# A decoder layer on one core: the build-time scheduler holds loads back and lets urgent operations pass, the first norm's weight vector is spread on chip, and the last tiles are transposed as they become final

## The chip, the cores and the metric

The kernel runs on one core of one Trainium2 chip. The metric is the device time of one execution in microseconds (us), as the median of three runs: 2298.27 (2297.4 to 2301.95). Lower is better.

## The reference

One layer of a hybrid decoder in float32. 16 learned meta tokens stand ahead of 1024 tokens; D = 1024, the feed-forward width is 2816, and there are 8 attention heads and 8 RWKV-7 heads of 64.

```python
h = concatenate([meta, x])                                   # 1040 x 1024
n = rms_norm(h, ffn1_norm);  h = h + 0.5 * (silu(n @ wg1) * (n @ wu1)) @ wd1
n = rms_norm(h, mix_norm);   p = n @ w_in                    # q,k,v and the RWKV columns
h = h + concatenate([stick_breaking_attention(p), rwkv7_time_mix(p)]) @ w_out
n = rms_norm(h, ffn2_norm);  h = h + 0.5 * (silu(n @ wg2) * (n @ wu2)) @ wd2
return rms_norm(h, final_norm)[16:]                          # x * rsqrt(mean(x^2) + eps) * gain
```

The RWKV recurrence is sequential over tokens; the kernel computes it in chunks, and each chunk needs the inverse of small lower triangular blocks.

## The kernel before

**Tiling.** Activations stand transposed: features on the 128 partitions, tokens along the row. The tokens are two groups, A (16 + 512) and B (512), and each group two chunks of 256 or 272 columns. The stages are ffn1, the input projection with attention and RWKV, `w_out`, ffn2 and the final norm; group B's ffn1 is woven into group A's mixing, and so on, so that TensorE always has some dense product at hand. Every dense product is three matmuls (`mm3`): activations and weights are each split into a high part (rounded to fp32r) and the rest, and high x high, low x high and high x low are added in PSUM. So each weight block is loaded (`wraw`, 512 KB on SP's queue, two buffers), copied to `whi` on ACT and subtracted to `wlo` on DVE. In the names of the profile `pg` and `pu` are the gate and up products, `pd` the down product, `pwo` that with `w_out`, `nh` and `nl` the high and low part of a normed activation, `ah` and `al` those of the feed-forward's inner activation.

**What sets the order.** While the program is built, a list scheduler inside the kernel (class `Clock`) plays it through with costs of its own. The stages are generators with priorities. A TensorE operation is issued as its generator comes to it; operations of DVE, ACT, POOL and the DMA issues of SP go into one pending list per engine, and `catch_up` takes, of all those whose inputs are there, the one with the smallest key: its earliest start first, and then its level (URGENT, LOAD, PLAIN, LAZY, set by `with self.urgent()` and the like). What is written out is one fixed order per engine; on the chip each engine works through its own in that order, and waits where an input is late. `self.dma` is the time until which the played DMA queue is full, `self.port` that until which DVE or POOL holds the memory port which the two share.

**Start** (`xfirst`, `startup`, `block`). The first two blocks of 128 tokens are loaded, then the vector `ffn1_norm`, as a DMA that copies it to all 128 partitions (`g1b`, 512 KB). ACT squares and sums each block, DVE makes the inverse root (`bst`) and one operation per block multiplies by root and vector (`xn`), TensorE transposes it in 16 pieces (`pxn`), ACT and DVE split them (`nh`, `nl`), and the first gate product can run.

**The triangular solve** (`lanes`, eight times in the kernel, once per piece of RWKV work). The 16 x 16 blocks go out to memory and come back with one block per partition (`Ld`, `lt`); POOL inverts them in 15 steps of two operations (`ltmp<-lt,T` and `T<-T,ltmp`); the inverse goes out (`Td`, `Nd`) and comes back by 16 DMAs of a few KB (`t<-Td`, `tt<-Nd`) as blocks of larger matrices; TensorE then combines them in four rounds of small matmuls, `pw`, `pp`, `pz`, `pe`, with evictions by ACT and DVE between. `pG` (line 1411, in `prep`) are products of 128 x 128 that a later part of a piece's work takes.

**Norm sums** (`norm_add`, `norm_sums`). After each finished tile of 128 features ACT squares it (`nsq`), DVE adds it to `nacc`; the square of the last tile is not added but summed by TensorE from its own matmuls. `nps` (middle) and `fss` (end) are these matmuls with a matrix of ones.

**The end** (`last` in `ffn`, `hookE`, `final`). The last down products are made for feature tiles m = 0 to 7; tiles 4 to 7 of the last chunk come last of all. Then `final` takes the sums, makes the inverse root (`fst`), transposes all 16 pieces of the chunk back (`po<-ident,h2B`), and DVE multiplies each 128 x 512 half row by root and gain (`gfb`, a broadcast of `final_norm`) into `ot`, which is stored, 256 KB at a time.

## Time and profile before

| what | before |
|---|---|
| median of three runs | 2298.27 us (2297.4 to 2301.95) |
| the profiled execution: own time | 2300.61 us |
| its span in the trace | 2298.3 us |
| TensorE busy | 2244.2 us, 98% |
| DVE / ACT / POOL busy | 69% / 46% / 30% |
| mean DMA rate | 113 GB/s |

Engines in the rows: PE is TensorE's matmuls and PEld its weight loads; DVE, ACT and POOL are the vector, scalar and GpSimd engines; SP issues the DMAs. Nearly every operation is recorded by one helper and so carries its line, L99; a row is told by the names of the tiles, `out<-in`, with buffer numbers left out. A duration in brackets at a row's end is the time that the engine stood idle before it, and behind the arrow what ended that. An fp32 matmul that is not fp32r appears as two rows' worth of records (two instructions are "x4"). PEclk is the clock that TensorE was granted, as a share of 2.4 GHz.

### The profile page before, as it was taken

How to read it: one execution, taken by the hardware profiler on the slowest of the kernel's cores; microseconds unless marked ns; L12 is line 12 of the kernel's file. 1: busy time of each engine (PE TensorE's matmuls, PEld its weight loads, DVE VectorE, ACT ScalarE, POOL GpSimd, SP SyncE). 2: the span in 40 equal slices, each digit the busy share in tenths (PEclk: the TensorE clock that was granted, in tenths of full speed). 3: DMA queues.
4: the chain of work that ended last, by engine and by line, in shares of the span. 5: the costliest groups of instructions: out<-in, count | busy, mean ns of one | idle time of the engine just before them, and what ended most of it. 6: DMA issues, size and time to landing. Idle time of an engine off the chain costs nothing.

```text
span 2298.3 us, 41595 instructions
## 1 busy us (share of the span) xinstructions
PE 2244.2 (98%) x16339; PEld 1986.8 (86%) x16339; DVE 1579.3 (69%) x2605; ACT 1067.1 (46%) x2115; POOL 700.0 (30%) x786
## 2 busy tenths in 40 slices
PE   7999999999999999999999979999999999999998
PEld 7999999999878788778778977887877898898998
DVE  5788776585666655666576887646777566788775
ACT  5444444444444434555434545445666333344442
POOL 0255541003142231441012324413544011255540
PEclk9999999999999999999999989999999999999999
DMA  4642332545743232332546533324231533333322
GB/s 140 195 117 76 108 111 67 153 138 138 214 129 95 70 103 82 111 90 74 157 140 196 144 92 101 90 81 133 67 91 57 159 106 115 97 102 104 107 87 80
DMA packets 412103, 259.68 MB, mean 113 GB/s; under 512 B 45060, under 2 KB 396500, under 8 KB 411908
## 3 DMA queue, kind: packets, MB, share of 16 engines
q1 hardware_dynamic: 411908, 257.04, 38.4%
q8 instruction: 128, 2.10, 0.4%
q14 instruction: 67, 0.55, 0.1%
HBM read 222.99 MB, written 33.99 MB: 112 GB/s over the span
## 4 chain that ended last, share of the span: by engine, by line
PE 88%; DVE 6%; DMA 2%; ACT 2%; issue 1%; SPq 0%; DVEq 0%; ACTq 0%
PE pd L99 33%; PE pu L99 20%; PE pg L99 19%; PE pwo L99 3%; PE px L99 3%; PE po L99 2%; PE pz L99 2%; PE pat L99 2%; DVE wlo L99 2%; DVE ql L99 1%; PE pG L99 1%; ACT whi L99 1%; DVE cc L99 1%; PE psw L99 0%; SPq L99 0%
## 5 line engine op out<-in xcount | busy, mean ns | idle before, releaser
L99 ACT ACTIVATE whi<-wraw 128x1024 fp32r<-128x1024 f32 (+1 forms) x318 | 334.8, 1053 | 360.1 <-PE pd L99 222.9
L99 DVE TENSOR_TENSOR wlo<-wraw,whi 128x1024 fp32r<-128x1024 f32 (+1 forms) x318 | 425.9, 1340 | 102.5 <-ACT whi L99 98.9
L99 PE MATMUL pd<-ah,whi 128*128 128x512 f32 (+2 forms) x944 | 326.2, 346 | 1.4 <-DVE h L99 1.2
L99 PE MATMUL pd<-al,whi 128*128 128x512 f32 (+2 forms) x944 | 319.0, 338 | 2.1 <-DVE al L99 2.0
L99 PE MATMUL pd<-ah,wlo 128*128 128x512 f32 (+2 forms) x944 | 319.3, 338 | 0.0
L99 PE MATMUL pd<-nh,whi 128*128 128x256 f32 (+7 forms) x648 | 210.5, 325 | 1.6 <-DVE st L99 1.6
L99 PE MATMUL pu<-nh,whi 128*128 128x512 f32 (+3 forms) x584 | 210.1, 360 | 0.0
L99 PE MATMUL pd<-nh,wlo 128*128 128x256 f32 (+7 forms) x648 | 205.1, 316 | 0.4 <-DVE wlo L99 0.4
L99 PE MATMUL pd<-nl,whi 128*128 128x256 f32 (+7 forms) x648 | 205.2, 317 | 0.0
L99 PE MATMUL pu<-nh,wlo 128*128 128x512 f32 (+3 forms) x584 | 201.1, 344 | 4.1 <-DVE wlo L99 4.1
L99 PE MATMUL pg<-nh,whi 128*128 128x512 f32 (+3 forms) x544 | 200.9, 369 | 0.0
L99 PE MATMUL pu<-nl,whi 128*128 128x512 f32 (+3 forms) x584 | 200.5, 343 | 0.0
L99 PEld LDWEIGHTS pd<-ah,whi 128*128 128x128 f32 x944 | 177.7, 188 | 23.8 <-issue 2.9
L99 POOL TENSOR_TENSOR al<-sl,ah 128x512 fp32r<-128x512 f32 (+2 forms) x47 | 77.8, 1655 | 389.5 <-ACT ah L99 384.2
L99 PEld LDWEIGHTS pd<-al,whi 128*128 128x128 f32 x944 | 177.8, 188 | 20.7 <-DVE al L99 3.5
L99 PEld LDWEIGHTS pd<-ah,wlo 128*128 128x128 f32 x944 | 177.7, 188 | 20.5
L99 PE MATMUL pg<-nh,wlo 128*128 128x512 f32 (+3 forms) x544 | 191.4, 352 | 0.8 <-DVE wlo L99 0.8
L99 PE MATMUL pg<-nl,whi 128*128 128x512 f32 (+3 forms) x544 | 191.6, 352 | 0.2 <-DVE nl L99 0.2
L99 DVE SCALAR_TENSOR_TENSOR h<-pd,h 128x256 f32<-128x256 f32 (+1 forms) x200 | 107.2, 542 | 68.2 <-PE pd L99 66.0
L99 PEld LDWEIGHTS pd<-nh,whi 128*128 128x128 f32 (+2 forms) x648 | 120.2, 186 | 14.4 <-issue 3.2
L99 POOL TENSOR_TENSOR qs<-wraw 128x512 f32<-128x512 f32 x60 | 93.5, 1559 | 117.9 <-DVE ql L99 41.3
L99 PEld LDWEIGHTS pd<-nh,wlo 128*128 128x128 f32 (+2 forms) x648 | 120.3, 186 | 9.3 <-DVE wlo L99 0.6
(379 smaller groups left out, 5759.3 us busy)
## 6 DMA issues: line engine op xcount, KB each, us to landing
wraw<-in_ffn_w_gate_dram SPq DMA_DIRECT2D x92, 512.0 KB
wraw<-in_ffn_w_up_dram SPq DMA_DIRECT2D x92, 512.0 KB
wraw<-in_ffn_w_down_dram SPq DMA_DIRECT2D x88, 512.0 KB
wraw<-in_w_in_dram SPq DMA_DIRECT2D x54, 512.0 KB
wraw<-in_w_out_dram SPq DMA_DIRECT2D x18, 512.0 KB
s<-rkvd SPq DMA_DIRECT2D x18, 256.0 KB
raw<-qkvd SPq DMA_DIRECT2D x16, 264.0 KB
raw<-qkvd SPq DMA_DIRECT2D x16, 256.0 KB
```

The lines of the kernel that those rows point to most:

```text
L99: self._c.trace(self._n, op, lambda: f(*a, **k), out, [x for x in args if isinstance(x, bass.AP)], k)
```

## The change

It has six parts.

1. *Scheduler.* In `catch_up` a DMA's key is now at least `self.dma - 3.0`: a transfer is held in the pending list until the played queue is nearly empty, so that one that turns up later can still go ahead of it. And every operation of the urgent level has 0.1 taken off its key, so that it goes ahead of one that could start a little sooner.
2. *RWKV's transfers are urgent*: `s<-rkvd`, `tw`, `Ld`, `lt`, `Td`, `Nd`, `t<-Td`, `tt<-Nd`.
3. *Start.* `ffn1_norm` is loaded as one row (4 KB), two fp32 matmuls with ones spread it over the partitions, and two DVE copies make `g1b`. For the first two blocks DVE multiplies the block by `g1b` while ACT still sums squares, and by the root afterwards (`TENSOR_SCALAR`); the second block's transposes take two more PSUM banks. A one-column `Square` on ACT comes first of all.
4. *Gain of the final norm* is one of the per-feature vectors, `vec`, and ACT multiplies `h` by it in place, after squaring (32 more ACT operations of 128 x 256); the load of `gfb` is gone, and the output of the other chunks is scaled on ACT (`final`).
5. *The last chunk* has `final_last`: a tile's two transposes are issued as it becomes final, the squares of its last three tiles are summed by TensorE rather than added on DVE, and the output goes as two DMAs of 128 x 1024, half of each scaled on DVE and half on ACT. Two of the PSUM banks of ffn2's last phase are set aside for it (8 to 6).
6. `norm_sums` waits for each of its sources just before it is used.

```diff
-                    key = (max(t, c, self.port if o.port else 0.0), o.prio)
+                    key = (max(t, c, self.port if o.port else self.dma - BACKLOG if e == "s" else 0.0)
+                           - AHEAD * (o.prio[0] == -self.URGENT), o.prio)      # AHEAD = 0.1, BACKLOG = 3.0
...
-                if s["k"] == KT - 1 and now and not s["tile"]:
-                    s["last"] = sq
+                if s["k"] >= KT - s["late"] and now and not s["tile"]:
+                    s["last"].append(sq)
...
-        yield self.need(*src, bank=next or self.nextbank)
+        yield self.need(*src[:1], bank=next or self.nextbank)
         ps = bank(name)
         for i, x in enumerate(src):
+            if i:
+                yield self.need(x)
...
-                nc.scalar.activation(xn, xt, AF.Square, accum_out=st[:, 0, j:j + 1])
+                nc.scalar.activation(hot[j] if hot else xn, xt, AF.Square, accum_out=st[:, 0, j:j + 1])
+                if hot:
+                    nc.vector.tensor_tensor(out=xn, in0=xt, in1=self.g1b, op=ALU.mult)
...
+                if hot:
+                    nc.vector.tensor_scalar(out=xn, in0=xn, scalar1=st[:, 2, j:j + 1], scalar2=None, op0=ALU.mult)
+                else:
+                    nc.vector.scalar_tensor_tensor(xn, xt, st[:, 2, j:j + 1], self.g1b[0:m], ALU.mult, ALU.mult)
...
-        for r, c, l in blks:
-            nc.sync.dma_start(out=Ld[l].rearrange("l s t -> s l t"), in_=ab[r, :, c])
+        with self.urgent():
+            for r, c, l in blks:
+                nc.sync.dma_start(out=Ld[l].rearrange("l s t -> s l t"), in_=ab[r, :, c])
...
+    def final_last(self, s, h2, cs, bank, early):
...
+        for m in range(KT):
+            yield lambda: s()["k"] > min(max(m, m // 4 * 6), KT - 1)
+            yield self.need(h2[:, m, cs])
+            for b in range(2):
+                if m % 4 == 0:
+                    if m:
+                        yield self.need(bank=self.nextbank)
+                    pts.append((bank if m else early)("po"))
+                    self.hold(pts[-1:])
+            for b in range(2):
+                nc.tensor.transpose(out=pts[m // 4 * 2 + b][:, m % 4 * P:m % 4 * P + P], in_=h2[:, m, cs.start + b * P:cs.start + b * P + P],
+                                    identity=self.ident)
+        st, _ = yield from self.norm_sums(s(), 256, "fss", bank)
+        yield lambda: hasattr(self, "fo")
+        for b in range(2):
+            ot = self.fo.tile([P, D], F32, name="ot%d" % b)
+            with self.urgent():
+                nc.vector.tensor_scalar(out=ot[:, 0:512], in0=pts[b], scalar1=st[:, 1, b:b + 1], scalar2=None, op0=ALU.mult)
+                nc.scalar.activation(ot[:, 512:D], pts[2 + b], AF.Copy, scale=st[:, 1, b:b + 1])
+                nc.sync.dma_start(out=self.out[0, 512 + cs.start + b * P:512 + cs.start + b * P + P, :], in_=ot)
...
             with self.urgent():
+                nc.sync.dma_start(out=g1r, in_=A["ffn1_norm"])
                 xs.extend(xload(0, *b) for b in blks[:2])
-                nc.sync.dma_start(out=self.g1b, in_=A["ffn1_norm"][0].partition_broadcast(P))
+                nc.scalar.activation(g1w, self.ones[:, 0:1], AF.Square)
+            for q in range(2):
+                yield self.need(g1r, bank=self.tbank)
+                ps = tb("pg1")
+                nc.tensor.matmul(ps, lhsT=self.ones[0:1, :], rhs=g1r[:, 512 * q:512 * q + 512], start=True, stop=True)
+                with self.urgent():
+                    nc.vector.tensor_copy(out=self.g1b[:, 512 * q:512 * q + 512], in_=ps)
...
+                if gain:
+                    x = hh[:, m, slice(*ch[i])]
+                    nc.scalar.activation(x, x, AF.Copy, scale=self.v(gain, m))
```

Since the scheduler's key decides between all pending operations, part 1 moves instructions through the whole middle of the program: about 80% of TensorE's rows, 67% of DVE's and 68% of SP's stand in the same order as before. The order of ffn2's blocks of dense products at the end of the program is unchanged up to its last tiles.

**DVE at the start of the program**, before and with the change (`bst` is the chain for the inverse root, `pg_177` and `pg_179` the spread vector in PSUM):

```order
L99 TENSOR_SCALAR bst<-bst 128x2 x2
...
L99 SCALAR_TENSOR_TENSOR bst<-bst 128x2
L99 SCALAR_TENSOR_TENSOR xn<-xt,bst,g1b 128x1024 x2
L99 TENSOR_TENSOR wlo<-wraw,whi 128x1024
L99 TENSOR_TENSOR nl_149<-pxn,nh_147 128x4x128
L99 TENSOR_TENSOR nl_150<-pxn,nh_148 128x4x128
L99 TENSOR_TENSOR wlo<-wraw,whi 128x1024
```

```order
L101 COPY g1b<-pg_177 128x512
L101 COPY g1b<-pg_179 128x512
L101 TENSOR_TENSOR xn<-xt,g1b 128x1024 x2
L101 TENSOR_SCALAR bst<-bst 128x2 x2
...
L101 TENSOR_TENSOR wlo<-wraw,whi 128x1024
L101 TENSOR_SCALAR xn<-xn,bst 128x1024 x2
L101 TENSOR_TENSOR wlo<-wraw,whi 128x1024
L101 TENSOR_TENSOR nl_149<-pxn,nh_147 128x4x128
```

The product with the vector has moved ahead of the chain for the root, and two weight blocks' `wlo` now stand ahead of the first `nl`, one of them between that chain and the last step of `xn`.

**POOL at the sixth solve**, before and with the change (`nl<-nf,nh` is the split of a normed activation; the last pair of the inversion is `ltmp<-lt,T 64x15` and `T<-T,ltmp 64x15`):

```order
L99 TENSOR_TENSOR ltmp<-lt,T 64x15
L99 TENSOR_TENSOR nl_149<-nf,nh_147 128x256 x2
L99 TENSOR_TENSOR nl_150<-nf,nh_148 128x256 x2
L99 TENSOR_TENSOR T<-T,ltmp 64x15
L99 TENSOR_TENSOR a<-a,kkn 128x512
```

```order
L101 TENSOR_TENSOR ltmp<-lt,T 64x15
L101 TENSOR_TENSOR T<-T,ltmp 64x15
L101 MEMSET t_15372 128x256
L101 MEMSET tt 128x1024
L101 MEMSET dec 128x8
L101 TENSOR_TENSOR a<-a,kkn 128x512
```

The last step of the inversion no longer stands behind the four splits. On TensorE, between that solve's second and third round, before and with the change:

```order
L99 MATMUL pp<-tt,lw 16x16 x32
L99 MATMUL pp<-lw,tt 32x16 x16
L99 MATMUL pz<-t_15604,ab 32x32 x16
L99 MATMUL pG<-x_15621,bk 128x128
L99 MATMUL pG<-x_15622,bk 128x128
```

```order
L101 MATMUL pp<-tt,lw 16x16 x32
L101 MATMUL pp<-lw,tt 32x16 x16
L101 MATMUL pwo<-nh_147,whi 128x256
L101 MATMUL pwo<-nl_149,whi 128x256
...
L101 MATMUL nps<-ones,nacc 128x1 x2
L101 MATMUL pz<-t_15372,ab 32x32 x16
L101 MATMUL nps<-ones,nsq 128x1 x2
```

Before, `pz` stands directly behind `pp`; with the change 24 matmuls `pwo` and one pair of norm sums stand between the two, and the second pair behind `pz`.

**TensorE at the end of the program**, before and with the change:

```order
L99 MATMUL pd<-ah,whi 128x256
L99 MATMUL pd<-al,whi 128x256
L99 MATMUL pd<-ah,wlo 128x256
L99 MATMUL fss<-ones,nacc 128x1 x2
L99 MATMUL fss<-ones,nsq 128x1 x2
L99 MATMUL po<-ident,h2B 128x128 x16
```

```order
L101 MATMUL pd<-ah,wlo 128x256
L101 MATMUL po<-ident,h2B 128x128 x2
L101 MATMUL pd<-ah,whi 128x256
L101 MATMUL pd<-al,whi 128x256
...
L101 MATMUL po<-ident,h2B 128x128 x4
L101 MATMUL fss<-ones,nacc 128x1 x2
L101 MATMUL fss<-ones,nsq 128x1 x6
```

Of the 16 transposes `po` that stood behind everything, 12 now stand between the down products `pd`, and the four of tiles 6 and 7 stand ahead of the sums, which have eight matmuls in place of four.

## Rows read from the trace of the kernel before

**Rows 1.** The page's first and fourth part: each engine's busy time, its share of the span and its instructions; and the shares, by engine, of the chain of work that ended last.
```profile
PE 2244.2 (98%) x16339; PEld 1986.8 (86%) x16339; DVE 1579.3 (69%) x2605; ACT 1067.1 (46%) x2115; POOL 700.0 (30%) x786
PE 88%; DVE 6%; DMA 2%; ACT 2%; issue 1%; SPq 0%; DVEq 0%; ACTq 0%
```

**Rows 2.** One kind of TensorE's waits, those for the low part of a weight block, summed: us in total, times, the longest.
```profile
PE pu L99 <- DVE wlo L99: 4.1, 3, 2.8
```

**Rows 3.** Stretches of the span: from and to (us), length, busy us (and instructions) of PE, PEld, DVE, ACT and POOL, granted clock, DMA share, GB/s. 610 to 618 follows a group of `pG`; 1328 to 1338 holds the norm sums and 1350 to 1358 the matmuls at the sixth solve; 2294 to 2295 lies in the last stores.
```profile
610.00:618.00 8.00, 7.20 (x41) 6.85 (x42) 6.39 (x12) 0.00 (x0) 0.00 (x0) 0.57 0.36 111
1328.00:1338.00 10.00, 5.83 (x30) 5.55 (x29) 9.74 (x18) 4.79 (x12) 4.99 (x8) 0.66 0.22 62
1350.00:1358.00 8.00, 3.29 (x165) 2.92 (x165) 5.66 (x13) 4.45 (x13) 0.96 (x2) 1.00 0.52 141
...
2294.00:2295.00 1.00, 0.00 (x0) 0.00 (x0) 0.00 (x0) 0.00 (x0) 0.00 (x0) 0.50 1.05 387
```

**Rows 4.** The timeline of all engines from the span's start: start (us), duration, engine (SPq is SP's issue of a DMA), operation, tiles, shapes, count, idle time before.
```profile
2.19 0.43 SPq L99 DMA_DIRECT2D g1b<-in_ffn_norm_dram  x1
...
4.84 1.28 ACT L99 ACT_TABLE_LOAD   x1 [4.84 <-DMA xt<-in_x_dram]
...
8.35 0.37 DVE L99 TENSOR_SCALAR bst<-bst 128x2 f32<-128x2 f32 x2 [8.35 <-ACT xn L99]
...
9.93 2.48 DVE L99 SCALAR_TENSOR_TENSOR xn<-xt,bst,g1b 128x1024 f32<-128x1024 f32 x2
...
11.36 1.94 PE L99 MATMUL pxn<-ident,xn 128*128 128x128 f32 x8 [11.36 <-DVE xn L99]
12.33 1.22 DVE L99 TENSOR_TENSOR wlo<-wraw,whi 128x1024 fp32r<-128x1024 f32 x1
...
13.46 1.28 DVE L99 TENSOR_TENSOR nl<-pxn,nh 128x512 fp32r<-128x512 f32 x2
...
14.21 1.97 PE L99 MATMUL pxn<-ident,xn 128*128 128x128 f32 x8 [0.90 <-DVE nl L99]
...
16.80 0.58 PE L99 MATMUL pg<-nl,whi 128*128 128x256 f32 x1 [0.21 <-DVE nl L99]
...
17.18 0.42 PE L99 MATMUL pg<-nh,wlo 128*128 128x256 f32 x1
...
17.40 0.42 PE L99 MATMUL pg<-nh,whi 128*128 128x256 f32 x1
```

**Rows 5.** Groups of equal operations over the whole span, by form: count, busy us in all, mean ns of one, idle us before.
```profile
L99 DVE TENSOR_SCALAR acc<-sw 128x640 f32<-128x640 f32 x2 | 1.0, 486 | 0.0
L99 PE MATMUL psa<-tw 32*128 32x320 f32 x8 | 3.2, 480 | 0.0
```

**Rows 6.** POOL's timeline at the sixth solve.
```profile
1312.82 0.62 POOL L99 TENSOR_TENSOR ltmp<-lt,T 64x15 f32<-64x15 f32 x1
1327.49 1.60 POOL L99 TENSOR_TENSOR nl<-nf,nh 128x256 fp32r<-128x256 f32 x2 [14.05 <-ACT nh L99]
...
1335.59 0.65 POOL L99 TENSOR_TENSOR T<-T,ltmp 64x15 f32<-64x15 f32 x1
```

**Rows 7.** SP's issues there: the inverse goes out, and the last of the 16 small loads that bring it back.
```profile
1336.27 0.49 SPq L99 DMA_DIRECT2D Td<-T  x1
...
1348.90 0.43 SPq L99 DMA_DIRECT2D tt<-Nd  x1
```

**Rows 8.** TensorE's timeline: a group of `pG` products, then the norm sums and the rounds of the sixth solve.
```profile
607.61 1.16 PE L99 MATMUL pG<-x,bk 64*128 64x128 f32 x14 [0.78 <-DVE x L99]
610.03 0.46 PE L99 MATMUL pG<-x,bk 64*128 64x128 f32 x2 [1.27 <-DVE bg L99]
611.25 2.04 PE L99 MATMUL pG<-x,bk 64*128 64x128 f32 x14 [0.76 <-DVE bg L99]
...
1330.56 0.92 PE L99 MATMUL nps<-ones,nacc 128*128 128x1 f32 x4 [2.24 <-DVE nacc L99]
1333.40 1.01 PE L99 MATMUL nps<-ones,nsq 128*128 128x1 f32 x4 [1.92 <-ACT nsq L99]
...
1351.34 0.68 PE L99 MATMUL pw<-t,ab 32*32 32x16 f32 x58 [1.78 <-DMA t<-Td]
...
1356.72 0.24 PE L99 MATMUL pz<-t,ab 32*32 32x32 f32 x2 [2.33 <-DVE t L99]
1358.29 1.06 PE L99 MATMUL pz<-t,ab 32*32 32x32 f32 x30 [1.32 <-DVE t L99]
```

**Rows 9.** The end: TensorE's timeline (the chunk before the last has its 16 transposes at 2281.08, between down products), then ACT's and DVE's.
```profile
2281.08 1.95 PE L99 MATMUL po<-ident,h2B 128*128 128x128 f32 x16
...
2286.66 0.28 PE L99 MATMUL pd<-ah,wlo 128*128 128x256 f32 x1
2288.40 0.58 PE L99 MATMUL fss<-ones,nacc 128*128 128x1 f32 x4 [1.47 <-DVE nacc L99]
...
2289.29 3.16 PE L99 MATMUL po<-ident,h2B 128*128 128x128 f32 x16
...
2287.49 0.42 ACT L99 ACTIVATE nsq<-h2B 128x256 f32<-128x256 f32 x1 [0.52 <-DVE h2B L99]
...
2289.46 0.16 DVE L99 TENSOR_SCALAR fst<-fss 128x2 f32<-128x2 f32 x1 [1.21 <-PE fss L99]
...
2291.12 2.73 DVE L99 SCALAR_TENSOR_TENSOR ot<-po,fst,gfb 128x512 f32<-128x512 f32 x4
```

More of the change, by code (lines that the diff above doesn't have):

```diff
@@ L706, in consts2 @@
         pv = psp.tile([P, 512], F32, tag="t", bufs=2, name="pv")
-        nc.tensor.transpose(out=pv[:, 0:50], in_=rows, identity=self.ident[0:50, 0:50])
-        self.vec = cp.tile([P, 50], F32, name="vec")
-        nc.vector.tensor_copy(out=self.vec, in_=pv[:, 0:50])
-        self.omv = cp.tile([P, 50], F32, name="omv")
+        nc.tensor.transpose(out=pv[:, 0:58], in_=rows, identity=self.ident[0:58, 0:58])
+        self.vec = cp.tile([P, 58], F32, name="vec")
+        nc.vector.tensor_copy(out=self.vec, in_=pv[:, 0:58])
+        self.omv = cp.tile([P, 58], F32, name="omv")
         nc.vector.tensor_scalar(out=self.omv, in0=self.vec, scalar1=-1.0, scalar2=1.0, op0=ALU.mult, op1=ALU.add)
@@ L719, in om, with norm_begin @@
         return self.omv[0:n, i:i + 1]
-    def norm_begin(self, tile=None):
-        return dict(k=0, tile=tile)
+    def norm_begin(self, tile=None, late=1):
+        return dict(k=0, tile=tile, late=late, last=[])
     def norm_add(self, s, h, k, cols, now=True):
@@ L1486, in lanes @@
         tmp = rp.tile([nl, 64], F32, tag="ltmp", name="ltmp")
-        nc.sync.dma_start(out=lt, in_=Ld)
+        with self.urgent():
+            nc.sync.dma_start(out=lt, in_=Ld)
         E = nc.gpsimd
@@ L1497, in lanes @@
         nc.scalar.activation(lt.rearrange("l c i -> l i c"), T, AF.Copy, scale=-1.0)
-        nc.sync.dma_start(out=Td, in_=T)
-        nc.sync.dma_start(out=Nd, in_=lt)
+        with self.urgent():
+            nc.sync.dma_start(out=Td, in_=T)
+            nc.sync.dma_start(out=Nd, in_=lt)
         yield lambda: free()
@@ L1508, in lanes @@
         for r, c, l in blks:
-            nc.sync.dma_start(out=t1[r, :, r.start % 32:r.start % 32 + B], in_=Td[l].rearrange("l i c -> i l c"))
-            nc.sync.dma_start(out=tt[r, :, r], in_=Nd[l].rearrange("l c i -> c l i"))
+            with self.urgent():
+                nc.sync.dma_start(out=t1[r, :, r.start % 32:r.start % 32 + B], in_=Td[l].rearrange("l i c -> i l c"))
+                nc.sync.dma_start(out=tt[r, :, r], in_=Nd[l].rearrange("l c i -> c l i"))
         lw = rp.tile([P, Q * 48], F32, tag="lw", name="lw")
@@ L2061, in some @@
                 out = lambda j, q: [n[2 + c][q][:, :, blks[js[j]][0]:blks[js[j]][0] + m] for c in range(2)]
-                yield from self.block([xs[j] for j in js], m, xp, tb, out, js[0] == 0)
+                hot = [xp.tile([P, KT, P], F32, tag="rb", bufs=2, name="xq").rearrange("p k t -> p (k t)") for j in js] if js[0] == 0 else None
+                yield from self.block([xs[j] for j in js], m, xp, tb, out, hot)
                 for j in js:
@@ L2184, in quads @@
                 p_.release()
+            if nm == "ffn2":
+                self.fo = pool("fo", bufs=1, side="right")
             yield lambda: nm == "ffn1" and c[0].quiet() or F.get(("fin1", 0)) and F.get(("fin1", 1)) and c[0].quiet()
+            if nm == "ffn2":
+                self.fo.release()
             c[0].release()
@@ L2230, in director @@
             ck.spawn(pieces(f2["h"], self.h1d[1]), 4)
-            nc.sync.dma_start(out=self.gfb, in_=A["final_norm"].partition_broadcast(P))
         def poll(f=None):
@@ L2294, in sumtile @@
                 return fsum[-1]
-            addF = add("fin0", h, chB, tile=sumtile)
+            addF = add("fin0", h, chB, tile=sumtile, gain="gf")
             def done(m):
```

55 lines of the change are left out of this document (32 added, 23 removed).

## The prediction

> **What bounds the kernel now.** I read the page's busy shares and its chain of waits first. TensorE is busy 2244.2 of 2298.3 us and has 88% of the chain that ended last, while DVE, the next, is busy 69% [rows 1]. So an operation added to DVE or ACT costs nothing unless TensorE waits for it, and nothing that the change does shortens TensorE's dense work. What can be won is TensorE's 54.1 us of idle time, and the time in which it works at half its clock after standing idle. I then read TensorE's waits and its timeline, to see where these lie.
>
> - Start: 11.36 us before the first transpose [rows 4].
> - Sixth solve: 2.24 and 1.92 us for norm sums, then 1.78 for the small loads and 2.33 and 1.32 for an eviction [rows 8], 9.6 in all. Around the sums the clock column falls to 0.66; around the rounds TensorE is busy 3.29 of 8 us [rows 3].
> - A group of `pG` at 607 to 611: 0.78, 1.27 and 0.76 us [rows 8], 2.8 in all, with a clock of 0.57 after it [rows 3].
> - The end: the last down product is over at 2286.94, and of the 11.4 us behind it TensorE works about 4.0 (0.9 of sums, from 2288.40 to 2289.29, and 3.16 of `po`) [rows 9], so 7.4 are idle.
> - All else: 54.1 - 11.4 - 9.6 - 2.8 - 7.4 = 22.9 us, in many small pieces, the largest kind of which is a wait for the low part of a weight block, 4.1 us in three places [rows 2].
>
> **The change part by part.**
>
> *Start: +1.0 us (-0.9 to +2.8).* Removed is the vector's 512 KB load; added are two fp32 matmuls, two copies and two products on DVE. `g1b` was no bound: DVE began its root at 8.35, released by ACT, and `xn` followed at 9.93 [rows 4]. Now the row must land (its issue stands first, where that of `g1b` stood at 2.19; at the latest 4.84, when the first big block was there [rows 4]; I take 2.6). The price of an fp32 matmul of 512 columns isn't in the trace. Nearest is a record of 320 columns at 0.48 us [rows 5], two records to an instruction, so 1.6 x 2 x 0.48 = 1.5 each, 3.1 for both, and twice that at the half clock; records overlap (products of 0.42 follow each other every 0.22 [rows 4]), so half of it is the lower end. So `g1b` is there between 4.8 (2.6 + 1.6 + 0.6 for the last copy) and 9.4; I take 7.3, the half clock with much overlap, since the first gate products take 0.42 us [rows 4] where the last down products take 0.28 [rows 9]. From there DVE works a queue: two products 2.44 (at 1.22, the row of `wlo`), the root 1.58 (8.35 to 9.93), a `wlo` 1.22 [rows 4], two scalings 1.56 (0.486 for 640 columns [rows 5], so 0.78 for 1024; 1.24 at most, by `xn` before), another `wlo` 1.22 and three `nl` of 0.64 [rows 4], 1.92: 9.94 together, and some 0.4 of waiting for transposes. The first product with `nl` then runs at 7.3 + 10.3 = 17.6, less 0.2 to 0.5, since not all of the three `nl` stands behind it, against 16.80 [rows 4], so 0.3 to 0.6 later, and with all waits between the engines I take 1.0. With `g1b` at 9.4 it is 19.6, +2.8; with 4.8 DVE would wait for the sums of squares as before, and 15.9, -0.9, is the least. The two further PSUM banks remove the 0.90 us wait between the two sets of transposes [rows 4], which lies inside this count. The early table load (1.28) is off the path, because DVE ends last. The 16 transposes stay ahead of the gate products, and those run at the slow step afterwards as now.
>
> The 16 transposes at 2281.08, between down products, took 1.95 us, 0.12 each, and at 11.36 and 14.21 eight took 1.94 and 1.97, 0.24 each [rows 4, 9]. The Trainium skill (TensorE: Matmul & The Clock Gate, Part 4: PE-mode transpose) says that transposes don't count as TensorE work for the clock. By that rule the eight transposes set closer together here bring the full clock no earlier, which is how I count; without it the slow stretch that follows could be about 0.9 us shorter. The trace agrees so far that the products after 3.9 us of transposes still start slow.
>
> *Sixth solve: -7 us (-14 to +2).* Before, the last step of the inversion stood behind four splits on POOL, which waited for a norm: its partner ran at 1312.82, it itself at 1335.59, 22.8 us later [rows 6]. Only then could the inverse go out (1336.27) and the 16 loads follow, the last issued at 1348.90, 12.6 us later [rows 7], so that `pw` still waited 1.78. In the new order the last step follows its partner directly, the loads aren't mixed with 512 KB weight loads, 24 products `pwo` of 0.11 (2.6 us; half the 0.22 at which products follow each other at the slow clock [rows 4]) stand between `pp` and `pz`, which before waited 2.33 and 1.32, and the norm sums stand apart. All of this is worth at most 9.6 us of waits, and the clock: about 2.0 behind the sums (15 products of `pg` at 0.22 a step and not 0.11, and the sums at 0.9) and 2.5 behind `pz` (the `pG` at 2.04 in place of 1.16, and 16 products), 14 in all. I take half. Late next are the norm sums themselves: DVE was busy 9.74 of 10 us there [rows 3], and the change moves none of that work away; and each of the 16 loads takes SP 0.43 us [rows 7], so 7 us for all.
>
> *`pG` group: -3.5 us (-5.4 to +1).* The 16 products are split into eight, 18 products `pu`, and eight. 18 x 0.11 = 2.0 us cover what the second half waited for. At stake are 2.8 of waits and 2.6 of clock (0.9 on the 14 at 2.04, 1.7 on 16 products). The first wait of 0.78 remains likely, and part of the clock with it.
>
> *End: +2.8 us (+1.2 to +4.5).* Twelve transposes now run among down products, where TensorE isn't idle: 12 x 0.12 = 1.4, and some 0.3 for the changes between them. Before, `fst` started 2.5 us after the last down product (2289.46) [rows 9]. Now the tile is added (0.4), squared on ACT (0.42), multiplied by its gain on ACT (priced like the square, 0.42), two transposes follow, and 16 records of sums where 8 were (those eight took 0.89 us, 0.11 each): 0.5 + 0.42 + 0.5 + 0.25 + 1.8 = 3.5, with the waits between engines 3.7, so `fst` is 1.2 later. After it, four `ot` on DVE took 2.73 us; two on DVE and two on ACT beside them take 1.4, so 1.3 is won. But the stores run at 387 GB/s [rows 3]: 1 MB is 2.7 us whichever way, and before they overlapped with `ot`, from the first of four on. Now the first 512 KB wait for a whole row (0.7) and the second for another 0.7. Their data end about 1.1 us later against the last down product than before. 1.7 + 1.1 = 2.8. The low end is without that 1.1 and with 0.5 less for the transposes, the high end lets each of the four hand-overs between engines cost 0.4 more.
>
> *The rest of the reordering: 0 (-8 to +10).* 22.9 us of small waits are dealt anew. A fair share of TensorE's rows moves, and no row says which way. The ends are a third won, and nearly half as much again lost with the clock that goes with it. The 32 gain operations (13 us of ACT at 0.42, ACT being busy 46%), the dropped `gfb` load, the two banks fewer and the outputs on ACT cost nothing in the middle: ACT has half its time idle there, and the dense order of ffn2 is unchanged. If that cover were gone, each gain operation would cost 0.42.
>
> Sum: 1.0 - 7 - 3.5 + 2.8 + 0 = -6.7. The profiled execution took 2300.61, 2.3 above the median of the runs; the same difference on the median gives 2298.3 - 6.7 = **2291.6**. A measurement of this kernel can tell about 0.2%, 4.6 us, from no change; so this is faster, by 0.3%.
>
> **The rivals.**
>
> *The rest takes it back (within 0.2%).* The solve's waits are won but appear elsewhere, since POOL's splits that now come later are needed by the next gate products. For it: waits for `wlo` and norm sums are by DVE, busy 69% in the mean and 97% there [rows 1, 3], and the change gives DVE no less to do. Against: the move of the last step takes nothing from any engine. With -3 for the solve, -1 for `pG` and +1 for the rest: 1 - 3 - 1 + 2.8 + 1 = +0.8, so 2299.
>
> *The urgent small loads starve the weights (slower).* At each of the eight solves 16 small loads stand in a row on SP, 16 x 0.43 = 6.9 us [rows 7], with no weight load between them, and held-back weight loads come later still. A block of weights lasts TensorE 24 products of 0.11, 2.6 us, and two buffers 5.3. If the buffers are not full when the loads begin, TensorE waits 1.6 us per solve, as long as the loads outlast the buffers, and eight times that is 13. It decides from the point at which a weight block lands over 5.3 us late. Against it: only 4.1 us of waits for `wlo` are in the whole trace [rows 2], and part of the solves stand where no weight is due. 2291.6 + 13 = 2304.6.
>
> *The ends gain as they are meant to.* If the fp32 matmuls run at the full clock, DVE's scalings at the low price, and the stores aren't bound by the rate, then start and end are -0.9 and +1.2 in place of +1.0 and +2.8, and with -9 for the solve it is -12: 2286.
>
> **How the numbers follow.** My forecast has 0.50: some 0.42 of it faster by over 0.2%, 0.08 within. The first rival has 0.22, all within 0.2%. The second has 0.20, slower. The third has 0.08, faster. Faster 0.50, same 0.30, slower 0.20. The forecast's own range is 2285 to 2298. For 8 in 10 the range runs on to the first rival and into the second: **2285 to 2302**. Left out are the upper part of the second rival (0.12) and the far end of the gains (0.08).
>
> **What would show it.** At the sixth solve: `T<-T` right behind its `ltmp`, `Td` some 20 us before `pw`, no wait above 0.5 us at `pz`, a clock near 1. At `pG`: one wait under 1 us. At the start: the first `pg<-nl` at 17 to 18. At the end: `fst` 3.5 to 4 us after the last `pd` and the data of the stores 1 us later after it than now. I am wrong if the waits of TensorE sum to as much as before in the middle, or if new waits for `wlo` stand at the solves.

## The result: 0.6% faster, twice the forecast

The changed kernel took 2285.68 us (median of four runs, 2283.59 to 2289.04), the kernel before 2299.37 beside it: a ratio of 0.9941 (95% interval 0.9923 to 0.9959). The forecast was 2291.6 and its range 2285 to 2302: the sign and the range held, the range only just (by the ratio, on the 2298.27 us that the forecast started from, it would be 2284.7, outside it), and the gain was 13.7 us where 6.7 had been summed. The profiled execution of the change spans 2285.4 us, 12.9 less than before, and that difference is taken apart here.

The page of the changed kernel (busy time, then shares of the chain that ended last):

```profile
PE 2242.8 (98%) x16351; PEld 1982.2 (87%) x16351; DVE 1563.0 (68%) x2593; ACT 1093.9 (48%) x2162; POOL 704.6 (31%) x786
PE 87%; DVE 6%; DMA 2%; ACT 2%; issue 1%; SPq 1%; POOL 0%; DVEq 0%; ACTq 0%; POOLq 0%
```

Against [rows 1] the busy shares say nothing: TensorE's is 98% again. What speaks is a sum of four parts per execution: TensorE's waits between the first gate product and the last down product, added up from its timeline; the time in that stretch at half the granted clock, from the first full step on (it counts half); the part behind the last down product; and what is left. The last hardly differs, since the products are the same:

| profiled execution | span | waits | at half clock | behind the last product | left |
|---|---|---|---|---|---|
| before | 2298.3 | 33.7 | 27.3 | 11.4 | 2223.6 |
| change | 2285.4 | 24.0 | 23.9 | 11.0 | 2222.3 |

(The column "left" is the time from the first gate product, at 16 us in both, to the last down product, less the waits and half of the time at half clock. The 24.6 us of waits that expectations below name for the change count one wait of 0.5 us twice.) So of 12.9 us, 9.7 are waits, 1.7 the clock, 0.4 the end, and 1.2 what is left. Those 1.2 are the start, where the full clock came 4.0 us after the first gate product before and 1.1 in the change: half of that difference is 1.4. By place, comparing the moments at which both have done the same amount of dense products: the change is 5.6 us ahead at 220 us, 9.5 at 1243, 12.9 at 1956, 14.2 at 2256, and 12.5 at the last.

One execution can be lucky with its clock, but the span and the mean granted clock of every run are on record. Their product is the span as it would be at full clock, and its mean over all runs is 2271.0 for the change and 2278 to 2280 for the kernel before (beside each group of runs below). So 7 to 9 of the 13.7 us are waits and order, and about 5 are clock, which was granted at 0.9942 in the mean and at 0.9920 to 0.9925 before.

**Start**, the timeline of the change (answers to [rows 4]):

```profile
2.38 3.75 PE L101 MATMUL pg<-g1r,ones 1*128 1x512 f32 x4 [2.38 <-DMA g1r<-in_ffn_norm_dram]
...
6.89 2.36 DVE L101 TENSOR_TENSOR xn<-xt,g1b 128x1024 f32<-128x1024 f32 x2
...
11.77 1.41 DVE L101 TENSOR_SCALAR xn<-xn,bst 128x1024 f32<-128x1024 f32 x2
...
12.57 3.67 PE L101 MATMUL pxn<-ident,xn 128*128 128x128 f32 x16 [6.44 <-DVE xn L101]
...
16.80 0.53 PE L101 MATMUL pg<-nl,whi 128*128 128x256 f32 x1
...
17.18 0.28 PE L101 MATMUL pg<-nh,wlo 128*128 128x256 f32 x1
```

The vector is spread by 6.85, close to my 7.3, and the first product with `nl` comes at 16.80, exactly as before. But the product at 17.18 takes 0.28, at the full clock, where before 0.42 stood there and the full step came at 19.96.

**The sixth solve**, three timelines (POOL's, SP's and TensorE's; answer to [rows 6 to 8]):

```profile
1294.08 0.62 POOL L101 TENSOR_TENSOR ltmp<-lt,T 64x15 f32<-64x15 f32 x1
1294.78 0.21 POOL L101 TENSOR_TENSOR T<-T,ltmp 64x15 f32<-64x15 f32 x1
```

```profile
1292.53 11.88 SPq L101 DMA_DIRECT2D wraw<-in_w_out_dram  x4
1304.52 0.52 SPq L101 DMA_DIRECT2D Td<-T  x1
...
1316.88 0.43 SPq L101 DMA_DIRECT2D tt<-Nd  x1
```

```profile
1317.67 0.68 PE L101 MATMUL pw<-t,ab 32*32 32x16 f32 x58 [0.24 <-DMA t<-Td]
...
1324.41 0.61 PE L101 MATMUL nps<-ones,nacc 128*128 128x1 f32 x4 [0.69 <-DVE nacc L101]
1325.86 1.07 PE L101 MATMUL pz<-t,ab 32*32 32x32 f32 x32 [0.84 <-DVE t L101]
1328.13 1.01 PE L101 MATMUL nps<-ones,nsq 128*128 128x1 f32 x4 [1.20 <-ACT nsq L101]
```

The last step of the inversion starts 0.7 us and not 22.8 after its partner, the loads no longer mix with weights, and 1.78, 2.33, 1.32, 2.24 and 1.92 us of waits have become 0.24, 0.84, 0.69 and 1.20. (`Td` still stood 9.5 us behind its data on SP, behind four weight loads whose issues took 11.88 us.) Counting every wait of 0.45 us or more from 1280 to 1400 us, 11.7 became 5.3.

**The `pG` group**, timeline of TensorE (answer to [rows 8]):

```profile
598.83 0.49 PE L101 MATMUL pG<-x,bk 64*128 64x128 f32 x2
601.70 2.07 PE L101 MATMUL pG<-x,bk 64*128 64x128 f32 x14 [2.38 <-DVE x L101]
...
613.28 1.16 PE L101 MATMUL pG<-x,bk 64*128 64x128 f32 x14 [0.61 <-ACT gate L101]
```

The first half now waits 2.38 us for DVE and not 0.78; the second, behind the products `pu`, 0.61 and not 2.03.

**The end**, timeline of TensorE, then of DVE and ACT (answers to [rows 9]):

```profile
2274.24 0.38 PE L101 MATMUL po<-ident,h2B 128*128 128x128 f32 x2
2275.91 0.44 PE L101 MATMUL po<-ident,h2B 128*128 128x128 f32 x2 [1.29 <-ACT h2B L101]
2276.18 0.50 PE L101 MATMUL fss<-ones,nacc 128*128 128x1 f32 x4
2276.55 1.48 PE L101 MATMUL fss<-ones,nsq 128*128 128x1 f32 x12
```

```profile
2278.06 0.16 DVE L101 TENSOR_SCALAR fst<-fss 128x2 f32<-128x2 f32 x1 [3.20 <-PE fss L101]
...
2279.64 1.41 DVE L101 TENSOR_SCALAR ot<-po,fst 128x512 f32<-128x512 f32 x2
2279.70 1.27 ACT L101 ACTIVATE ot<-po,fst 128x512 f32<-128x512 f32 x2 [3.85 <-DVE fst L101]
```

The last down product ends at 2274.40; the root starts 3.66 us later (forecast 3.5 to 4) where before it was 2.5.

### The profile page after: what moved, and what is told of

It reads as the page before. It is cut to its first block, busy times and chain, and to the rows that moved or that the text cites. A ratio compares the mean times of both kernels' runs of the same rounds, so it can differ in the third digit from the quotient of the medians.

```text
span 2285.4 us, 41628 instructions
## 1 busy us (share of the span) xinstructions
PE 2242.8 (98%) x16351; PEld 1982.2 (87%) x16351; DVE 1563.0 (68%) x2593; ACT 1093.9 (48%) x2162; POOL 704.6 (31%) x786
## 4 chain that ended last, share of the span: by engine, by line
PE 87%; DVE 6%; DMA 2%; ACT 2%; issue 1%; SPq 1%; POOL 0%; DVEq 0%; ACTq 0%; POOLq 0%
PE pd L101 33%; PE pu L101 20%; PE pg L101 19%; PE px L101 3%; PE pwo L101 3%; PE po L101 2%; PE pz L101 2%; DVE wlo L101 2%; PE pat L101 2%; DVE ql L101 1%; SPq L101 1%; ACT whi L101 1%; PE pG L101 1%; DMA wraw<-in_ffn_w_down_dram 1%; DMA wraw<-in_ffn_w_up_dram 1%
## 5 line engine op out<-in xcount | busy, mean ns | idle before, releaser
L101 PEld LDWEIGHTS pd<-nh,whi 128*128 128x128 f32 (+2 forms) x648 | 120.1, 185 | 12.5 <-issue 3.1
L101 POOL TENSOR_TENSOR qs<-wraw 128x512 f32<-128x512 f32 x60 | 92.9, 1548 | 111.5 <-DVE ql L101 41.1
```

The lines of the kernel that those rows point to most:

```text
L101: self._c.trace(self._n, op, lambda: f(*a, **k), out, [x for x in args if isinstance(x, bass.AP)], k)
```

## The experiments

Of every run that follows, the ratio is to the kernel before on the same chip. The columns are those of the table above; the last is the mean over all runs of span times granted clock (before 2278.4 to 2279.5, the change 2271.0). In that one half clock behind the last product counts too, and that ahead of the first full step does not, so differences under 2 us aren't read.

| run | median us | ratio (95%) | span | waits | at half clock | behind | left | at full clock |
|---|---|---|---|---|---|---|---|---|
| e1_warm | 2300.3 | 0.9991 to 1.0011 | 2299.7 | 30.5 | 37.6 | 11.3 | 2222.8 | 2278.4 |
| e4_sched | 2295.81 | 0.9975 to 0.9995 | 2297.0 | 28.0 | 34.1 | 10.0 | 2225.5 | 2278.6 |
| e5_oldstart | 2286.36 | 0.9930 to 0.9955 | 2284.6 | 25.5 | 17.1 | 11.1 | 2223.1 | 2274.4 |
| e6_oldtail | 2277.72 | 0.9894 to 0.9919 | 2277.3 | 23.4 | 13.7 | 8.9 | 2222.1 | 2269.5 |
| e7_fill | 2283.65 | 0.9922 to 0.9947 | 2281.5 | 23.0 | 6.8 | 11.0 | 2227.8 | 2272.0 |
| e8_oldrules | 2291.02 | 0.9954 to 0.9977 | 2290.0 | 30.8 | 20.5 | 11.5 | 2221.5 | 2274.9 |
| e9_nohold | 2294.57 | 0.9973 to 0.9992 | 2297.0 | 32.0 | 30.7 | 11.5 | 2222.2 | 2277.0 |
| e10_noahead | 2289.2 | 0.9942 to 0.9972 | 2287.1 | 28.8 | 20.5 | 11.0 | 2220.9 | 2273.7 |
| e2_noturgent | 2311.09 | 1.0037 to 1.0070 | 2307.8 | 41.1 | 44.4 | 11.7 | 2216.8 | 2281.1 |
| e3_hold4 | 2290.07 | 0.9942 to 0.9972 | 2288.0 | 26.5 | 20.5 | 11.7 | 2222.5 | 2270.2 |
| e11_sums | 2283.91 | 0.9913 to 0.9946 | 2276.7 | 25.0 | 3.4 | 9.3 | 2224.5 | 2269.6 |
| e12_stores | 2284.85 | 0.9923 to 0.9956 | 2282.1 | 23.2 | 17.1 | 11.0 | 2223.2 | 2271.0 |

### The start: e1_warm and e5_oldstart

```diff
+        warm = tb("pwarm").rearrange("p (a b) -> p a b", a=4)
+        for _ in range(2):
+            nc.tensor.matmul(warm, lhsT=self.ones[0:1, :], rhs=self.ones[0:1, :].unsqueeze(1).to_broadcast([1, 4, P]), start=True, stop=True)
```

> The kernel before with one addition: two fp32 matmuls of 128 x 512 on constants, whose result nobody reads, stand first on TensorE; every other instruction and its order is unchanged. Theory (clock): with the change the first gate product with the low part ran at 16.80 us as before, but TensorE's full clock came at 17.2 and not at 19.85, because the matmuls that spread the weight vector had run from 2.4 to 6.1. Then this kernel has its full clock by about 17 us too, the first products stay at 16.0 and 16.8, and it is 1.3 to 2.7 us faster than before. Rival (the transposes, set closer together in the change, bring the clock): no change at the start, full clock at 19.85, time within 0.5 us of before.

TensorE's timeline of e1_warm:

```profile
1.58 3.77 PE L2041 MATMUL pwarm<-ones 1*128 1x512 f32 x4 [1.58 <-POOL ones L664]
...
18.63 0.39 PE L99 MATMUL pg<-nh,wlo 128*128 128x256 f32 x1
18.85 0.29 PE L99 MATMUL pg<-nh,whi 128*128 128x256 f32 x1
```

The early matmuls ran as in the change, but the full clock came at 18.9, between the 19.96 of before and the theory's 17, and the time did not move, at full clock neither (2278.4 as before). So early work alone is not the cause: this theory fell as it was put.

e5_oldstart is the changed kernel with `xfirst`, `startup` and `block` as before:

```diff
...
             with self.urgent():
-                nc.sync.dma_start(out=g1r, in_=A["ffn1_norm"])
                 xs.extend(xload(0, *b) for b in blks[:2])
+                nc.sync.dma_start(out=self.g1b, in_=A["ffn1_norm"][0].partition_broadcast(P))
...
```

> The changed kernel with the start of the kernel before (the weight vector by a 512 KB transfer, one operation per block for the norm, two PSUM banks for the transposes); the order of everything behind the start is that of the changed kernel. Theory (clock): 2.3 to 2.7 us slower than the changed kernel, all of it in the first 45 us, with the first product with the low part at 16.8 and the full clock near 19.9. Rival (my forecast of the start, the change costs 1.0): 1.0 us faster than the changed kernel.

Rows of e5_oldstart's TensorE timeline:

```profile
18.17 0.28 PE L101 MATMUL pg<-nh,wlo 128*128 128x256 f32 x1
...
35.37 0.66 PE L101 MATMUL px<-ident,xt 128*128 128x128 f32 x4 [0.82 <-DVE nl L101]
...
105.14 0.38 PE L101 MATMUL pg<-nh,wlo 128*128 128x256 f32 x1 [0.76 <-DVE wlo L101]
```

By the row at 117 us of the change it is 3.4 us behind: 1.6 by 34 us (the first product 0.3 later, the full clock at 18.2, a wait of 0.82), the rest in longer waits at 105 and 120 us. So my forecast's sign fell. The theory had 2.3 to 2.7 us, all in the first 45 us, with the full clock near 19.9: more was lost, but half of it later, and the clock came at 18.2. In the median it can't be seen (2286.36), because the clock was better later on: in this execution it stood at half for 17.1 us and not 23.9, which is 3.4 us back. At full clock, over all runs, the old start is 3.4 us slower (2274.4 and 2271.0).

Of the ten profiled executions with the new start, eight had the full step 0.9 to 2.4 us after the first gate product (the change 1.1), and two, e2_noturgent and e12_stores, 0.5 and 0.6 us *before* it; the four with the old start had it 1.8 to 4.0 us after. In e12_stores (the transposes up to 15 us and from 15.3 on, with their shortest, middle and longest duration in ns; then the timeline):

```profile
L101 PE MATMUL pxn<-ident,xn x11: 417/417/473, 12.7 to 14.9; 128*128 128x128 f32 x11
L101 PE MATMUL pxn<-ident,xn x4: 272/292/414, 15.3 to 15.8; 128*128 128x128 f32 x4
```

```profile
12.68 3.36 PE L101 MATMUL pxn<-ident,xn 128*128 128x128 f32 x16 [6.45 <-DVE xn L101]
16.19 0.39 PE L101 MATMUL pg<-nh,whi 128*128 128x256 f32 x1
```

There a transpose goes from 0.42 to 0.27 us at about 15.5 us, behind 6.45 us of idle time and 2.9 us of nothing but transposes. So transposes do bring the full clock here. That the new start has it sooner because its 16 stand without a pause (3.67 us in the change), in place of eight, a pause and eight, fits this, but is not shown: the new PSUM banks weren't tried alone, and executions of one start differ by 2 to 3 us.

### The scheduler: e4_sched, e8_oldrules, e9_nohold, e10_noahead, e2_noturgent, e3_hold4

e4_sched has parts 1 and 2 on the kernel before (the key of `catch_up` with its two constants and the urgent level of RWKV's transfers, and nothing else); the other five start from the changed kernel:

```diff
-AHEAD = 0.1        # e8_oldrules, e10_noahead
+AHEAD = 0.0
-BACKLOG = 3.0      # e8_oldrules, e9_nohold: out of reach; e3_hold4: 4.0
+BACKLOG = 1e9
-            with self.urgent():      # e8_oldrules, e2_noturgent: RWKV transfers plain again (one of the places)
-                nc.sync.dma_start(out=t1[r, :, r.start % 32:r.start % 32 + B], in_=Td[l].rearrange("l i c -> i l c"))
+            nc.sync.dma_start(out=t1[r, :, r.start % 32:r.start % 32 + B], in_=Td[l].rearrange("l i c -> i l c"))
```

> The kernel before with parts 1 and 2 of the change alone: the scheduler's key (transfers held back, urgent operations 0.1 ahead) and the urgent level for the transfers of the RWKV part. Start and end stand in the order of the kernel before. Theory (the reordering carries the gain): of the 12.9 us by which the profiled span is shorter, the start has 2.5 and the end costs 1.3, so this kernel is 11 to 12 us faster than before (about 2288), without the wait of 2.8 us at 101.8. Rival (start, end and the two parts work only together, since each moves the order of all that follows): 3 to 8 us faster.

> The changed kernel without parts 1 and 2 (no transfers held back, no 0.1 ahead, the transfers of the RWKV part not urgent); start, gain, end and the waits per source are those of the change. Theory (the scheduler's new key wins the idle time, -9 us of waits): waits of TensorE behind the start of 31 to 34 us, as before the change, and 2293 to 2298. Rival (any shift of the planner's times deals the waits anew, and the changed kernel is a lucky draw): anything, with waits as few as 25 us possible, 2283 to 2290.

> The changed kernel without holding transfers back (the planner's bound on the queue is out of reach); urgent operations still go 0.1 ahead, and the rest is the change. Theory (holding back is what lets the small loads of the solves go first): waits of TensorE rise from 24.6 to about 30 us, 2290 to 2295. Rival (the head start of urgent operations carries it): waits stay at 24 to 26 us, 2283 to 2288.

> The changed kernel without the 0.1 head start of urgent operations; transfers are still held back. Theory (the head start lets evictions on DVE pass the long weight splits, and so removes small waits all over): waits of TensorE rise from 24.6 to about 30 us, 2290 to 2295. Rival (holding back carries it): waits stay at 24 to 26 us, 2283 to 2288.

> The changed kernel with the transfers of the RWKV part at the plain level again; transfers are held back and urgent operations go 0.1 ahead as in the change. Theory (the urgent level is what brings the inverse of a solve back in time): the waits of TensorE from 1280 to 1400 us rise from 5.3 to 7.5 us or more, with one of over 1 us for the small loads, and the kernel takes 2288 to 2294. Rival (held-back weight loads leave the queue free anyway): waits and time as in the changed kernel, 2283 to 2288.

> The changed kernel with transfers held back until the planned queue has 4.0 and not 3.0 us left. Theory (the rule lowers the waits, whatever the exact order): waits of TensorE behind the start of 24 to 27 us, as in the three kernels with both parts and the new end, and 2283 to 2288. Rival (the changed kernel's order is a lucky draw): waits of 28 us or more, 2289 or more.

Neither part is worth its share alone. With the old rules and all else new (e8) the waits are 30.8 us; with head start and urgent loads but nothing held back (e9) 32.0; with holding and urgent loads but no head start (e10) 28.8; with all three 24.0. At the solve e8 waits again for the small loads, 3.25 us, and for a weight block's low part, 2.81 (TensorE's waits there):

```profile
1324.55 0.39 PE L101 MATMUL pwo<-nh,wlo 128*128 128x256 f32 x1 [2.81 <-DVE wlo L101]
...
1348.26 0.68 PE L101 MATMUL pw<-t,ab 32*32 32x16 f32 x58 [3.25 <-DMA t<-Td]
```

e9 waits there 1.04 and 1.77 us for the small loads, and e10 2.00 and 1.95 for the norm sums: at this solve each of the two rules takes away one kind. The waits of e8 and its 2291 us lie just under what the theory had (31 to 34, 2293 to 2298), those of e10 too (28.8 for 30, 2289.2 for 2290 to 2295), e9's within it.

Holding back without urgency (e2) is the worst of all, slower than before by 0.4 to 0.7%. Its waits, by kind, and the two longest in the timeline:

```profile
PE pu L101 <- DVE wlo L101: 7.2, 4, 4.7
...
PE pwo L101 <- DVE wlo L101: 5.4, 2, 5.1
PE pg L101 <- DVE wlo L101: 4.4, 2, 2.5
```

```profile
1917.29 0.58 PE L101 MATMUL pwo<-n2Bh,wlo 128*128 128x256 f32 x1 [5.13 <-DVE wlo L101]
...
1936.21 0.58 PE L101 MATMUL pu<-n2Bh,wlo 128*128 128x256 f32 x1 [4.72 <-DVE wlo L101]
```

Around the solve its waits came to 9.1 us, above the theory's 7.5, but none of them is for the small loads. At 1917 the weights come late: SP issued the last six `w_out` blocks ahead over 23.8 us and the next block only at 1908. My second rival, weights starved by the new rules, is thus real, but it comes when the RWKV loads are *not* urgent; why their level decides it at 1917, in a place without a solve, stays open.

Is the changed kernel's order a lucky draw? The changed kernel and the six made from it that keep the three rules have waits between 23 and 27, the four that lack one or all between 28.8 and 41.1. But the six are hardly draws of their own: told by their tiles, 99% and more of TensorE's rows stand in the change's order (with 4.0 us held, e3, 99.6%), of e8's 89%. e3 has the waits that the theory gave it (26.5) but 2290.07 us, above its 2288, by the clock: at full clock it is as fast as the change. The one other order with all three rules is e4_sched's, on the old frame (start and end as before), with waits of 28.0. It measured 0.05 to 0.25% faster, 34.1 us at half clock in its profile, but at full clock it gains nothing (2278.6, before 2278.4). My expectation of 11 to 12 us was wrong, the rival's 3 to 8 nearer. So in the new frame the rules are worth about 4 us at full clock (e8 2274.9, the change 2271.0), and in the old one nothing that can be told; whether it is the rules or this one order stays open.

### The clock behind the solve: e7_fill

```diff
...
+        fill(5, True)            # n fp32 matmuls, ones x ident, into ps[:, 256:384], in the sixth pair of sums alone
         for i, x in enumerate(src):
             if i:
+                fill(5, False)
                 yield self.need(x)
+                fill(6, False)
...
```

> The changed kernel with 16 fp32 matmuls of 128 x 128 columns on constants (into unused columns of the sums' bank) where TensorE waits around the last norm sums of the sixth solve: 5 ahead of the first sums, 5 behind them, 6 ahead of the second; all else in the same order. In the profile of the changed kernel TensorE waits 0.69, 0.84 and 1.20 us there, and then works some 12 us at half its clock. Theory (the solve's waits were won and the half clock behind the rest took it back): TensorE stays at its full clock there, the waits are filled and not shortened, and the kernel is about 4 to 6 us faster than the changed one, near 2280. Rival (the half clock there is chance and not tied to these waits): the half-clock stretches in the middle stay as many as before, time within 2 us of the changed kernel.

Windows of the change, of e6_oldtail (the same instructions in the same order up to the last tiles, its edit is below) and of e7_fill: from, to, length, busy us, and the granted clock as the third number from the end.

```profile
1330.00:1335.00 5.00, 5.00 (x51) 4.71 (x51) 2.94 (x8) 1.34 (x4) 0.00 (x0) 0.50 0.73 205
1335.00:1341.00 6.00, 6.00 (x30) 6.00 (x30) 3.65 (x11) 2.57 (x6) 0.00 (x0) 0.50 0.01 3
```

```profile
1330.00:1335.00 5.00, 5.00 (x62) 4.62 (x61) 3.46 (x12) 1.76 (x6) 0.00 (x0) 0.81 0.75 208
1335.00:1341.00 6.00, 5.22 (x44) 5.03 (x44) 5.63 (x16) 4.64 (x12) 0.73 (x1) 1.00 0.15 41
```

```profile
1330.00:1335.00 5.00, 5.00 (x68) 4.70 (x69) 4.54 (x14) 2.44 (x9) 0.00 (x0) 1.00 0.74 210
1335.00:1341.00 6.00, 5.19 (x45) 4.97 (x44) 5.63 (x15) 4.64 (x12) 0.79 (x1) 1.00 0.15 42
```

With the waits filled the clock stays at 1.00, as the theory has it, and it is the only one of the 14 profiled executions in which no half clock begins between 1322 and 1334 us. The fillers cost 1.28, 1.36 and 1.60 us of TensorE, so the net gain is small (ratio 0.9935 beside the change's 0.9941, not distinguishable), not 4 to 6 us. But the second triple says more: with the same waits (0.84 and 1.20) and the same order, the clock was back after 3.4 us in e6 and stayed at half for 13.7 in the change. So waits open the door to the half clock, and how long it lasts differs between executions: over the whole span 3.4 us of half clock in e11 and 23.9 in the change, with waits of 25.0 and 24.0. The Trainium skill (TensorE: Matmul & The Clock Gate, Part 1) says of the slow phase at a kernel's start that the same kernel shows different lengths of it in different runs. Here the same is seen in the middle.

### The end: e6_oldtail, e11_sums, e12_stores

```diff
-            addE = add("fin1", f2["h"], chB, gain="gf", late=(1, 3))      # e6_oldtail, with final_last left out
+            addE = add("fin1", f2["h"], chB, gain="gf")
-                if addE(i, m) and i == 0:
+                if addE(i, m):
...
+            if m == KT - 1:                                               # e11_sums, ahead of the last transposes
+                st, _ = yield from self.norm_sums(s(), 256, "fss", bank)
...
-                nc.sync.dma_start(out=self.out[0, 512 + cs.start + b * P:512 + cs.start + b * P + P, :], in_=ot)
+                for kk in range(2):                                       # e12_stores
+                    nc.sync.dma_start(out=self.out[0, 512 + cs.start + b * P:512 + cs.start + b * P + P, 512 * kk:512 * kk + 512], in_=ot[:, 512 * kk:512 * kk + 512])
```

> The changed kernel with the last chunk finished as in the kernel before: no transposes among the down products, one square summed by TensorE, 16 transposes behind the sums, four stores of 128 x 512; the gain stays on ACT and the scaling of the outputs is on ACT. The order ahead of the last tiles is that of the changed kernel. Forecast (the new end costs 2.8): 2.8 us faster than the changed kernel. Theory from the trace (the transposes and one wait delay the last down product by 1.7 us, and the span ends 0.4 us sooner after it): 1 to 1.5 us faster. Rival (the new end wins as it is meant to): 1 us or more slower.

> The changed kernel with one move at its end: the sums of squares stand ahead of the last tile's two transposes on TensorE, not behind them. In the changed kernel these transposes wait 1.29 us for ACT's gain, and the sums, whose sources are ready before, stand behind. Theory (that wait delays the end): the root starts about 0.9 us sooner after the last down product, and the part behind that product falls from 11.0 to about 10.1 us. Rival (the stores set the end): the end moves by less than 0.3 us.

> The changed kernel with the last chunk stored as four transfers of 128 x 512, as before the change, in place of two of 128 x 1024; all else in the same order. Theory (the two halves of a row are ready together, on DVE and on ACT, so a store of half a row starts no sooner): the part behind the last down product stays at 11.0 us within 0.3. My forecast (the first store waits 0.7 for the whole row): 0.7 us shorter.

The end of e6_oldtail, all engines; its last down product ends at 2268.35:

```profile
2268.36 0.61 PE L101 MATMUL fss<-ones,nacc 128*128 128x1 f32 x4
...
2269.31 0.61 PE L101 MATMUL fss<-ones,nsq 128*128 128x1 f32 x4 [0.35 <-ACT nsq L101]
2269.78 1.95 PE L101 MATMUL po<-ident,h2B 128*128 128x128 f32 x16
2269.96 0.16 DVE L101 TENSOR_SCALAR fst<-fss 128x2 f32<-128x2 f32 x1 [1.15 <-PE fss L101]
...
2271.59 2.42 ACT L101 ACTIVATE ot<-po,fst 128x512 f32<-128x512 f32 x4 [1.79 <-DVE fst L101]
2272.30 2.07 SPq L101 DMA_DIRECT2D out_dram<-ot  x4
```

The old order of the end has the best time of all: 2277.72 us, in each of its five runs below every one of the change's. In the traces it is 2.1 us shorter behind the last product (8.9 and not 11.0) and reaches that product 2.1 us sooner once the lead that it has before the end is set aside (4.0 us at 2250, 6.05 at the last product): 4.2 together, above the 1 to 1.5 of the theory and the 2.8 of the forecast. The lead of 4.0 before is clock, told above, and nothing in the edit explains it; by all runs, at full clock, the old end is only 1.5 us ahead (2269.5 and 2271.0), which that column hardly tells from nothing. So what the old end is worth is open, up to 4 us, and the 8 us between the medians are mostly clock. The transposes that the change moves ahead of the end hide behind the root here: `po` runs from 2269.78, the root's chain from 2269.96. e11 shows what the rest is: with the sums first the root starts 1.9 us after the last product (2267.42) and not 3.66, and the part behind falls to 9.3, twice the 0.9 expected, since the sums' own 1.8 us then lie beside the wait for the gain. e12 shows that the larger stores are not to blame: 10.96.

## Why the forecast was right in sign and half in size

- **Solve, -7 forecast.** The mechanism was right for the waits, 11.7 to 5.3. The clock term was not: around it TensorE worked 13.7 us at half clock before and 17.1 in the change, which gives 1.7 back. Measured about -4.7. Of the signs one came, `T` right behind its `ltmp`; `Td` went 13 us and not 20 before `pw`, `pz` waited 0.84 us and not under 0.5, and the clock behind was 0.50.
- **`pG`, -3.5 forecast.** The split of the 16 products did not pay: 3.0 us of waits stand where 2.8 stood, and the clock is at half for 6.8 us in both. Measured about 0. The products `pu` did cover most of the second half's wait (2.03 to 0.61). The step that failed is that the first wait stays at 0.78: it became 2.38, for DVE's `x`.
- **Start, +1.0 forecast.** The queue on DVE came out at 16.80, 0.8 under the sum, and the two things that the sum did not have were worth more than it: the full clock 2.8 us sooner, and the waits at 36 and 101.8 us gone (waits of 0.45 us or more up to 160 us went from 3.6 to 0.45 us, with a half-clock stretch behind 101.8). Measured -5.6 by 220 us. The sum left the clock out by the rule on transposes, which e12_stores contradicts, and the wait at 101.8 stood in it among the small waits of the rest. Not all of the 5.6 is the start's: with the old rules the new start has 5.0 of it (e8_oldrules), and with the old start the new rules have 1.8 (e4_sched).
- **End, +2.8 forecast.** Right in sign, too large: 2.1 us lost up to the last product (14.6 us of lead ahead of the last tiles, 12.5 at the product) where 1.7 were summed, and 0.4 won behind it where 1.1 were to be lost. The root is 1.1 later, as summed (1.2), and the outputs on two engines are 1.3 us shorter, as summed; the step that failed is that the rate of the stores takes this back. From the root to the end it is 7.4 us where before it was 8.8.
- **The rest, 0 (-8 to +10) forecast.** Measured about -4, as what the other four leave of -12.9: waits of 0.8 to 1.3 us gone at 501, 638 and 1900 us, others of 0.9 to 1.2 new at 522, 1480 and 1643, a half-clock stretch at 1098 gone (by chance: e6_oldtail, in the same order, has one at 1089).

So the solve brought the sign, as forecast, but more than half of the size came from the start and the rest, which the sum had at +1.0 and 0. That the time lies inside the range, at the third rival's 2286, is in part luck.

The first rival (the rest takes it back) did not come. The third (the ends gain) came at the start and not at the end. The second, weights that starve, was seen in e2_noturgent alone.

## What to carry to other kernels

When one engine is 98% busy, take a time apart into its waits, its time at half clock, and its two ends: what is left stayed between 2217 and 2228 us over 14 executions, and most edits show in one of the four. And set the clock aside over all runs before two kernels are compared: here it hid the 3.4 us of the start and made most of the lead of the old end. Rules of a list scheduler that hold work back need a level that lets the urgent go first: here holding back without it was slower than neither, and the level without holding back was no faster than neither. Work moved ahead of a kernel's end must be work that nothing there would have hidden: transposes that run beside another engine's chain, as in e6_oldtail, cost nothing there.

## What the runs showed of the hardware

The half clock was not bound to an order of instructions: behind the norm sums of the sixth solve, with one order and the same waits of 0.84 and 1.20 us, it lasted 3.4 us in two executions (e6_oldtail, e11_sums) and 13.7 in three (the change, e5_oldstart, e12_stores). That is 5 us of difference, and over the runs of one kernel the time varies by as much (2283.59 to 2289.04).

Transposes brought the full clock: in e12_stores and e2_noturgent it came while only they were running, 2.9 and 3.0 us after the first of them. The Trainium skill (TensorE: Matmul & The Clock Gate, Part 4: PE-mode transpose) says they don't count, and the forecast of the start went by it; these two executions speak against it for transposes by an fp32 matmul with the identity. A run in which nothing at all stands ahead of them is missing: the matmuls that spread the vector had ended 6.45 us earlier.
